# A two-layer decoder trunk on one core: compression input in two parts, MLP weights spread, first scores of layer 0 later, sparse-attention copies all on ScalarE

## The chip, the core and the metric

The kernel runs on one core of one Trainium2 chip. The metric is the device time of one execution in microseconds; the time before is the median of three runs. All detail comes from one further execution that was profiled.

## What is computed

x has 512 tokens of 1024 channels, in float32. Each of two layers normalises x, projects it to 5912 columns, runs two attentions side by side on the result, gates and merges them, and adds the output projection to x. Cut to what matters here:

```python
def hybrid_layer(x, pos, ...):
    h = rms_norm(x, norm_g)
    sb_q, sb_k, sb_v, sb_z, n_q, n_kc, n_vc, n_ks, n_vs, n_kw, n_vw, n_gate, n_z, gate_a, gate_b = split(h @ w_in)
    o_a = stick_breaking_attention(heads(sb_q), heads(sb_k), heads(sb_v))   # 8 heads
    y_a = merge_heads(o_a) * silu(sb_z)
    q = rope(rms_norm(heads(n_q)), pos)
    o_b = nsa_attention(q, ...)      # compressed, selected and window branches, 8 heads over 2 key groups
    y_b = o_b * silu(n_z)
    merged = sigmoid(gate_a) * (y_a @ w_up_a) + sigmoid(gate_b) * (y_b @ w_up_b)
    return x + merged @ w_out

def compress_blocks(x, idx, pe, w1, b1, w2):      # keys and values of the compressed branch
    blocks = x[:, :, idx] + pe                    # 31 blocks of 32 tokens, stride 16
    return silu(flat(blocks) @ w1 + b1) @ w2
```

Stick-breaking attention takes for each query the scores of earlier keys, a reversed cumulative sum of their log-sigmoids, and weights w from both. The sequence of 512 tokens is worked in blocks of 128 queries.

## The kernel before

A float32 product is split: a weight raw becomes whi (a rounded copy, from a cast on ScalarE or GpSimd) and wlo = raw - whi (on VectorE, line 408), the activations h become hh and hl, and TensorE adds three products, hh with whi, hl with whi and hh with wlo. So each projection is a row of matmuls of 512 columns, 24 for a block of 128 output columns, with raw loaded by SP's queue through a few rotating buffers (`w_load`, `w_split`, `w_get`). The matmuls of the value projections (`proj_tok`) go the other way round, with 256 columns.

The order of the work is written by a small planner while the program is built, in `Pacer`. It keeps a clock of its own in assumed microseconds; `pc.later(us, fn)` emits fn once that clock has advanced so far, and `pc.pump(us)` takes matmuls from a queue of fill work, `pc.fill`, until the clock has advanced by so much. The assumed delays are in `LAT`, `X_GAP`, `Y_GAP` and `Y_LAT`. On VectorE, ScalarE and GpSimd priorities (`tc.high_priority`) decide which of the instructions at hand goes first.

A layer has these stages.

- Start. In layer 0 x is loaded and transposed by TensorE into banks S; ScalarE copies them out (line 592), GpSimd and VectorE make hh and hl (lines 593, 594), and the first projections for stick-breaking (one pair of heads) run at once. r, the norm's factor, comes from a Ln and an Exp on ScalarE (lines 604, 605) and is broadcast into r_bc (line 621); a second Ln and Exp make an epsilon term (270, 271). sX and sK are the stacked operands of the scores; half of sK is moved to other partitions by a DMA that ScalarE issues (825, 826).
- X, the stick-breaking part. For t = 0 to 15, four heads' pairs times four query blocks, `sb_qk` makes the scores S, `sb_cs` the cumulative sums, and two steps later `sb_pv` makes the output o from w and the values gv. In each step ScalarE makes e = exp(S), its log, and w. Between these, fill work runs in the order of `X_FILL`: q, sq and sk are projections, cmp the two compressed projections, vs and vn the values, mlp 0 to 3 the four quarters of the compression MLP's hidden layer, k the keys of the sparse part. `LAT["sb0"]` is how long after the first projections the first scores are called for.
- `prep_cmp` (the cmp fill) evicts each projection into ct (line 687) and adds the position term pe to overlapping blocks, which gives f_t, the input of the compression MLP: per projection eight adds of 64 x 248 on VectorE (line 694), two key groups by two token parities by two halves of the block. `prep_mlp` multiplies f_t with the MLP weights (two loads per quarter). `prep_vs` evicts the values with VectorE into gv (line 663).
- Y, the sparse part. For u = 0 to 15 (four pairs of heads, j, times four query blocks, i), `nsa_qk` makes the scores of selected and window keys, VectorE their maxima mx (1047), ScalarE pr = exp (1052), VectorE scales pr (1060). `nsa_t` transposes pr on TensorE into tp and copies each block to SBUF as pT, blocks 0 and 2 on ScalarE (line 1074), 1 and 3 on VectorE (1076). `nsa_pv` multiplies pT with the values. Once per j, `cmp_qk` makes the compressed scores sc (to line 997), `cmp_t` transposes them and copies them to pcT on ScalarE (1006), and `cmp_pv` uses pcT. Gates and z projections are the fill here (`Y_FILL`).
- Merge and output projection, not touched.

The sine and cosine tables for the rotary embedding are made once, in layer 0, on ScalarE (`angles_sin`, lines 243 to 248). They need another table set of ScalarE than Exp and Ln do, so each Sin is ordered behind the last Ln instructions that the program has recorded so far in `lns`, and after them the Exp and Ln set is loaded by hand (line 141):

```python
sins = [A.activation(cos_t, cos_t, AF.Sin, bias=halfpi, scale=-1.0), ...]
for i in sins:
    for j in lns:
        order(i, j)
sin_tab.load, sin_tab.n = load_exp_ln(sins), 8
```

Where an instruction needs a set that is not active and nothing was loaded by hand, the compiler puts a load in (ACT_TABLE_LOAD with that instruction's line).

Of the kernel before, what the change touches and what calls it, by code (L numbers as in the profile page):

```python
# [17 lines left out]
AF = mybir.ActivationFunctionType  # L18
# [19 lines left out]
PRIO = 300  # L38
FIRST_R = 6
N_WARM = (3, 2, 2, 3)  # L40
LAT = {'norm': 5.0, 'mlp_t': 9.0, 'mlp_w2': 3.5, 'mlp_k': 16.0, 'sb0': 3.0, 'sb': 4.5, 'ang': 1.5, 'sin': 0.5}
PRIO_SB = 600
PRIO_EV = 900
X_GAP = (3.5, 3.4)
Y_GAP = 1.5
Y_LAT = (7.3, 6.9, 6.9, 8.8)
N_GATE = 13

# [2 lines left out]
def kernel(  # L51
# [20 lines left out]
    V, A, T, G = nc.vector, nc.scalar, nc.tensor, nc.gpsimd  # L72
# [54 lines left out]
    with tc.high_priority(offset=3000):  # L127
        pt = t_bank()
# [96 lines left out]
    def angles_load():  # L225
        pos_i = wk.tile([P, S], I32, tag="wk", name="pos_i")
        nc.sync.dma_start(pos_i, positions[0:1, :].to_broadcast([P, S]))
        pc.later(LAT["ang"], lambda: angles_reduce(pos_i))

# [116 lines left out]
    pc = Pacer()  # L346
# [170 lines left out]
    def tok_plan(l, p):  # L517
        return [("tok", l, p, 0), ("tok", l, p, 1)]

    X_FILL = [('q', 0), ('sq', 1), ('sk', 1), ('sq', 2), ('sk', 2), ('cmp', 0), ('vs', 1), ('mlp', 0), ('mlp', 1), ('sq', 3),  # L520
              ('sk', 3), ('k', 0), ('mlp', 2), ('k', 1), ('mlp', 3), ('vn', 0), ('q', 1), ('q', 2), ('q', 3)]
    Y_FILL = [("z", 0), ("g", 0), ("g", 1), ("g", 2), ("g", 3), ("z", 1), ("g", 4), ("g", 5), ("z", 2),
              ("g", 6), ("g", 7), ("z", 3)] + [("g", a) for a in range(8, N_GATE)]
# [118 lines left out]
    for l in range(depth):  # L642
# [3 lines left out]
        with ExitStack() as lc:  # L646
# [3 lines left out]
            done = set()  # L650
# [29 lines left out]
            def prep_cmp():  # L680
                for f in f_v:
                    V.memset(f[:, :, :, :, NCMP:], 0.0)
                for a, c in ((0, C_KC), (1, C_VC)):
                    po = yield from proj(l, "col", c)
                    ct = wkt("ct")
                    with tc.high_priority(offset=PRIO_EV):
                        V.tensor_mul(ct, po, r_bc)
                    for g in range(2):
                        gs = slice(g * HD, (g + 1) * HD)
                        pe_v = pe_t[gs, l, a].rearrange("p (k t) -> p k t", t=2)  # L690
                        for t in range(2):
                            src = ct[gs].rearrange("p (c k t) -> p k t c", k=8, t=2)
                            for hf in range(2):
                                V.tensor_tensor(  # L694
                                    f_v[hf][t * HD:(t + 1) * HD, :, a, g, 0:NCMP],
                                    src[:, :, t, hf:hf + NCMP],
                                    pe_v[:, hf * 8:(hf + 1) * 8, t:t + 1].to_broadcast([HD, 8, NCMP]),
                                    op=ALU.add)

            def prep_k(b):  # L700
                po = yield from proj(l, "col", (C_KS, C_KW)[b])
# [12 lines left out]
            mlp = H()  # L714
# [348 lines left out]
            def nsa_t(pr, i, gap):  # L1063
                pTs = []
                for kb in range(i + 1):
                    pt = t_bank()
                    ptv = pt.rearrange("p (g t q) -> p g t q", g=2, t=2)
                    for g in range(2):
                        for t in range(2):
                            tr(ptv[:, g, t], pr[g][:, kb, t], identf)  # L1070
                    pT = py.tile([P, 2, 2, P], F32, tag="pT", name="pT", bufs=NT)
                    with tc.high_priority(offset=PRIO_SB):
                        if kb % 2 == 0:
                            A.activation(pT.rearrange("p g t q -> p (g t q)"), pt, AF.Copy)  # L1074
                        else:
                            V.tensor_copy(pT.rearrange("p g t q -> p (g t q)"), pt)  # L1076
                    pTs.append(pT)
                    pc.pump(gap)
                return pTs
# [19 lines left out]
            with ExitStack() as lx:  # L1099
# [59 lines left out]
                eng.copy = copy_pool  # L1159
                sb_evac_q(R, po[0])  # L1160
                sb_evac_k(R, po[1])
                pc.later(LAT["sb0"], lambda: done.add(("sb", 0)))
                pc.fill.append(prep_vs(0))
                pc.fill.extend([fills[kind](a) for kind, a in X_FILL])
                NS = 4 * NT
# [18 lines left out]
            with ExitStack() as ly:  # L1184
                py = ly.enter_context(tc.tile_pool(name=f"py{l}", bufs=1, reuse_waits="tile"))
                pc.fill.extend([fills[kind](a) for kind, a in Y_FILL])
                sc = cmp_qk(0)
# [3 lines left out]
                for u in range(17):  # L1191
                    j, i = u // NT, u % NT
                    pc.pump(ready - pc.now)
                    if u > 0:
                        nsa_pv(o, pTs, (u - 1) % NT)
                        if i == 0:
                            nsa_o(j - 1, o)
                    if u == 16:
                        break
                    if u < 15:  # L1200
                        j2 = (u + 1) // NT
                        pc.until(lambda: j2 in n_in)
                        pr[u + 1] = nsa_qk(j2, (u + 1) % NT)
                        ready = pc.now + Y_LAT[(u + 1) % NT]
                        if i == 2 and j < 2:
                            pc.until(lambda: ("q", j + 2) in done)
                            set_nX(j + 2, n_q[j + 2])
                    if i == 0:
                        pcT = cmp_t(sc)
                    pTs = nsa_t(pr.pop(u), i, Y_GAP)  # L1210
                    if i == 0:
                        o = cmp_pv(pcT)
                    if i == 2 and j < 3:
                        pc.until(lambda: j + 1 in n_in)
                        sc = cmp_qk(j + 1)
# [110 lines left out]
```

## Time and profile before

| | |
|---|---|
| median of 3 runs | 1015.94 us (1014.74 to 1016.39) |
| the profiled execution | 1017.15 us, span 1015.4 us |
| TensorE busy | 980.1 us, 97%, 5379 matmuls |
| VectorE busy | 698.3 us, 69% |
| ScalarE busy | 444.9 us, 44% |
| GpSimd busy | 208.2 us, 21% |
| the chain that ended last | TensorE 75%, VectorE 16%, ScalarE 4%, DMA 2% |

The span is what the profile covers, from the first to the last instruction; the run's own time is 1.75 us longer. TensorE is PE in the profile, VectorE DVE, ScalarE ACT, GpSimd POOL. "Busy" counts a matmul to its modelled end, so neighbouring matmuls overlap; how fast TensorE works is better read from the distance of two starts.

### The profile page before, as it was taken

How to read it: one execution, taken by the hardware profiler on the slowest of the kernel's cores; microseconds unless marked ns; L12 is line 12 of the kernel's file. 1: busy time of each engine (PE TensorE's matmuls, PEld its weight loads, DVE VectorE, ACT ScalarE, POOL GpSimd, SP SyncE). 2: the span in 40 equal slices, each digit the busy share in tenths (PEclk: the TensorE clock that was granted, in tenths of full speed). 3: DMA queues.
4: the chain of work that ended last, by engine and by line, in shares of the span. 5: the costliest groups of instructions: out<-in, count | busy, mean ns of one | idle time of the engine just before them, and what ended most of it. 6: DMA issues, size and time to landing. Idle time of an engine off the chain costs nothing.

```text
span 1015.4 us, 14862 instructions
## 1 busy us (share of the span) xinstructions
PE 980.1 (97%) x5379; PEld 770.7 (76%) x5379; DVE 698.3 (69%) x1369; ACT 444.9 (44%) x1102; POOL 208.2 (21%) x256
## 2 busy tenths in 40 slices
PE   6999899999999999999999989999999999999997
PEld 5877767767777778888888776687777777788886
DVE  7778557889696876465565965687977776755631
ACT  4554446655243333623344533666534332345321
POOL 4152243621101101000014424352210110100000
PEclk9999899999999999999999989999999999999999
DMA  9333066432221212344643315463222121224341
GB/s 289 101 95 102 5 173 139 115 84 53 63 64 42 63 50 72 88 128 121 177 115 85 93 41 146 107 146 84 62 63 63 42 63 43 62 83 136 93 115 52
DMA packets 167530, 94.36 MB, mean 93 GB/s; under 512 B 39568, under 2 KB 160672, under 8 KB 167456
## 3 DMA queue, kind: packets, MB, share of 16 engines
q1 hardware_dynamic: 163120, 88.14, 32.3%
q10 hardware_dynamic: 3632, 3.17, 1.3%
q0 software_dynamic: 704, 2.11, 0.5%
q8 instruction: 42, 0.69, 0.3%
q14 instruction: 32, 0.26, 0.1%
HBM read 80.81 MB, written 6.29 MB: 86 GB/s over the span
## 4 chain that ended last, share of the span: by engine, by line
PE 75%; DVE 16%; ACT 4%; DMA 2%; issue 1%; POOL 1%; SPq 0%; DVEq 0%; POOLq 0%; ACTq 0%
PE acc L349 48%; PE S L349 16%; PE o L349 5%; PE tp L353 3%; DVE mx L1047 2%; DVE wlo L408 2%; DVE pr L1060 2%; ACT pr L1052 2%; PE tp L349 1%; DVE f_t L694 1%; DVE nX L509 1%; DMA raw<-in_w_in_dram 1%; DMA sK<-sK 1%; DMA mpos_i<-in_positions_dram 1%; DVE mx L1049 0%
## 5 line engine op out<-in xcount | busy, mean ns | idle before, releaser
L349 PE MATMUL acc<-hh,whi 128*128 128x512 f32 x640 | 256.9, 401 | 2.9 <-POOL whi L162 1.9
L349 PE MATMUL acc<-hl,whi 128*128 128x512 f32 x640 | 256.3, 401 | 1.7 <-DVE hl L594 1.4
L349 PE MATMUL acc<-hh,wlo 128*128 128x512 f32 x640 | 178.7, 402 | 0.0
L408 DVE TENSOR_TENSOR wlo<-raw,whi 128x1024 fp32r<-128x1024 f32 (+1 forms) x124 | 158.2, 1277 | 26.1 <-POOL whi L162 15.9
L162 POOL TENSOR_SCALAR whi<-raw 128x1024 fp32r<-128x1024 f32 (+1 forms) x84 | 98.5, 1174 | 374.3 <-PE acc L349 259.1
L349 PEld LDWEIGHTS acc<-hh,whi 128*128 128x128 f32 x640 | 121.2, 189 | 28.8 <-POOL whi L162 2.9
L349 PEld LDWEIGHTS acc<-hl,whi 128*128 128x128 f32 x640 | 120.9, 189 | 28.1 <-DVE hl L594 3.4
L349 PEld LDWEIGHTS acc<-hh,wlo 128*128 128x128 f32 x640 | 118.1, 189 | 26.5 <-issue 3.1
L408 ACT CAST whi<-raw 128x1024 fp32r<-128x1024 f32 x40 | 42.0, 1050 | 122.9 <-PE S L349 45.9
L1052 ACT ACTIVATE pr<-S,mx 128x256 f32<-128x256 f32 (+1 forms) x192 | 81.8, 446 | 32.0 <-DVE mx L1049 24.3
L1074 ACT ACTIVATE pT<-tp 128x512 f32<-128x512 f32 x48 | 28.7, 599 | 96.1 <-PE tp L353 95.8
L1047 DVE TENSOR_REDUCE mx<-S 128x2 f32<-128x512 f32 (+1 forms) x96 | 53.5, 594 | 20.6 <-PE S L349 20.4
L349 PE MATMUL acc<-whi,hh 128*128 128x256 f32 (+1 forms) x192 | 58.7, 306 | 6.0 <-DVE gv L663 6.0
L219 ACT ACTIVATE e<-S 128x128 f32<-128x128 f32 (+3 forms) x64 | 25.4, 435 | 86.6 <-DVE S L903 82.9
L353 PE MATMUL tp<-identf,pr 128*128 128x128 f32 x320 | 50.4, 278 | 9.4 <-DVE pT L1076 3.1
L349 PE MATMUL acc<-wlo,hh 128*128 128x256 f32 (+1 forms) x192 | 56.8, 296 | 0.0
L349 PE MATMUL acc<-whi,hl 128*128 128x256 f32 (+1 forms) x192 | 56.6, 295 | 0.0
L353 PEld LDWEIGHTS tp<-identf,pr 128*128 128x128 f32 x320 | 38.0, 141 | 21.8 <-ACT pcT L1006 6.5
L349 PE MATMUL S<-yh,wlo 128*128 128x512 f32 x128 | 50.8, 396 | 0.0
L349 PE MATMUL S<-yh,whi 128*128 128x512 f32 x128 | 50.7, 396 | 0.0
L1060 DVE TENSOR_SCALAR pr<-pr,rc 128x128 f32<-128x128 f32 (+3 forms) x128 | 49.3, 429 | 1.6
L349 PE MATMUL S<-yl,whi 128*128 128x512 f32 x128 | 50.1, 392 | 0.0
(315 smaller groups left out, 1784.3 us busy)
## 6 DMA issues: line engine op xcount, KB each, us to landing
raw<-in_w_in_dram SPq DMA_DIRECT2D x72, 512.0 KB, 3.8
raw<-in_w_in_dram SPq DMA_DIRECT2D x36, 256.0 KB, 3.8
raw<-in_cmp_w_dram SPq DMA_DIRECT2D x16, 512.0 KB, 4.4
raw<-in_w_out_dram SPq DMA_DIRECT2D x16, 512.0 KB, 4.0
raw<-in_w_up_a_dram SPq DMA_DIRECT2D x16, 256.0 KB, 3.1
raw<-in_w_up_b_dram SPq DMA_DIRECT2D x32, 128.0 KB, 3.3
gv<-xs SPq DMA_DIRECT2D x16, 256.0 KB, 2.7
sq<-xq SPq DMA_DIRECT2D x48, 64.0 KB, 2.0
```

The lines of the kernel that those rows point to most:

```text
L162: G.tensor_scalar(dst, src, 1.0, 0.0, op0=ALU.mult, op1=ALU.add)
L219: ins = A.activation(dst, src, func, **kw)
L349: T.matmul(out, lhsT, rhs, start=start, stop=stop, **kw)
L353: T.transpose(out, in_, ident)
L408: for ins in (eng.copy(hi, rv), V.tensor_sub(lo, rv, hi.bitcast(F32))):
L509: V.tensor_sub(X[b, g], q[a], X[a, g].bitcast(F32))
L694: V.tensor_tensor(f_v[hf][t * HD:(t + 1) * HD, :, a, g, 0:NCMP], src[:, :, t, hf:hf + NCMP], pe_v[:, hf * 8:(hf + 1) * 8, t:t + 1].to_broa ...
L1047: V.tensor_reduce(mx[:, hf, g], sbk[-1], axis=AX.XY, op=ALU.max, negate=True)
L1052: exps.append(A.activation(pr[g][:, a:b, t], sbk[hf][:, t], AF.Exp, bias=mx[:, 0, g, t:t + 1], accum_out=dn[:, hf, g, t:t + 1]))
L1060: V.tensor_scalar(pr[g][:, :nk, t], pr[g][:, :nk, t], rc[:, g, t:t + 1], None, op0=ALU.mult)
L1074: A.activation(pT.rearrange("p g t q -> p (g t q)"), pt, AF.Copy)
```

## The change

- `prep_cmp` emits the four adds of one key group's first half (`block(0)`) at once and those of the second half (`block(1)`) later, by a delay `F_GAP` on the planner's clock.
- In `X_FILL` the second MLP quarter goes behind the projection ('sq', 3).
- The first scores are called for after 6.0 instead of 3.0 in layer 0 and after 3.8 in layer 1.
- `nsa_t` copies every pT on ScalarE.
- `cmp_t` is called ahead of `nsa_pv` and `nsa_qk` instead of behind them.

```diff
-LAT = {'norm': 5.0, 'mlp_t': 9.0, 'mlp_w2': 3.5, 'mlp_k': 16.0, 'sb0': 3.0, 'sb': 4.5, 'ang': 1.5, 'sin': 0.5}
+LAT = {'norm': 5.0, 'mlp_t': 9.0, 'mlp_w2': 3.5, 'mlp_k': 16.0, 'sb0': 3.8, 'sb': 4.5, 'ang': 1.5, 'sin': 0.5}
+F_GAP = ((6.0, 8.0), (5.0, 7.0))
...
-    X_FILL = [('q', 0), ('sq', 1), ('sk', 1), ('sq', 2), ('sk', 2), ('cmp', 0), ('vs', 1), ('mlp', 0), ('mlp', 1), ('sq', 3),
+    X_FILL = [('q', 0), ('sq', 1), ('sk', 1), ('sq', 2), ('sk', 2), ('cmp', 0), ('vs', 1), ('mlp', 0), ('sq', 3), ('mlp', 1),
...
-                        for t in range(2):
-                            src = ct[gs].rearrange("p (c k t) -> p k t c", k=8, t=2)
-                            for hf in range(2):
+                        src = ct[gs].rearrange("p (c k t) -> p k t c", k=8, t=2)
+
+                        def block(hf, a=a, g=g, src=src, pe_v=pe_v):
+                            for t in range(2):
                                 V.tensor_tensor(
                                     f_v[hf][t * HD:(t + 1) * HD, :, a, g, 0:NCMP],
                                     src[:, :, t, hf:hf + NCMP],
                                     pe_v[:, hf * 8:(hf + 1) * 8, t:t + 1].to_broadcast([HD, 8, NCMP]),
                                     op=ALU.add)
+
+                        block(0)
+                        pc.later(F_GAP[a][g], lambda block=block: block(1))
...
-                        if kb % 2 == 0:
-                            A.activation(pT.rearrange("p g t q -> p (g t q)"), pt, AF.Copy)
-                        else:
-                            V.tensor_copy(pT.rearrange("p g t q -> p (g t q)"), pt)
+                        A.activation(pT.rearrange("p g t q -> p (g t q)"), pt, AF.Copy)
...
-                pc.later(LAT["sb0"], lambda: done.add(("sb", 0)))
+                pc.later(LAT["sb0"] if l else 6.0, lambda: done.add(("sb", 0)))
...
                     pc.pump(ready - pc.now)
+                    if i == 0 and u < 16:
+                        pcT = cmp_t(sc)
                     if u > 0:
                         nsa_pv(o, pTs, (u - 1) % NT)
...
-                    if i == 0:
-                        pcT = cmp_t(sc)
                     pTs = nsa_t(pr.pop(u), i, Y_GAP)
```

The change also moves instructions that it does not name. Three places follow; the line numbers of the changed kernel are one higher from line 46 on and up to five higher further down.

VectorE in layer 0, from the second compressed projection to the first eviction of values; f_t is the MLP's input in two tiles, ct the evicted projection, e a part of the stick-breaking scores. Before (the two kinds of add alternate four times where the dots stand):

```order
L903 TENSOR_TENSOR S<-S,mk_sb 128x128 x2
L687 TENSOR_TENSOR ct<-acc,r_bc 128x512
L907 SCALAR_TENSOR_TENSOR e<-S,e 128x384 x2
L694 TENSOR_TENSOR f_t_187<-ct,pe_t 64x8x31
L694 TENSOR_TENSOR f_t_188<-ct,pe_t 64x8x31
...
L663 TENSOR_SCALAR gv<-acc,r_col 128x256
L923 TENSOR_TENSOR sp<-e,sp 128x384 x2
L663 TENSOR_SCALAR gv<-acc,r_col 128x256
```

Now:

```order
L688 TENSOR_TENSOR ct<-acc,r_bc 128x512
L409 TENSOR_TENSOR wlo<-raw,whi 128x1024
L696 TENSOR_TENSOR f_t_187<-ct,pe_t 64x8x31 x2
L908 TENSOR_TENSOR S<-S,mk_sb 128x128 x2
L696 TENSOR_TENSOR f_t_187<-ct,pe_t 64x8x31 x2
L696 TENSOR_TENSOR f_t_188<-ct,pe_t 64x8x31
L664 TENSOR_SCALAR gv<-acc,r_col 128x256
L696 TENSOR_TENSOR f_t_188<-ct,pe_t 64x8x31 x2
L912 SCALAR_TENSOR_TENSOR e<-S,e 128x384 x2
L696 TENSOR_TENSOR f_t_188<-ct,pe_t 64x8x31
L664 TENSOR_SCALAR gv<-acc,r_col 128x256
```

All eight adds stood between ct and the first gv; now five do, with a wlo and an S pair, and three adds and the e pair follow gv.

ScalarE in layer 0's start, from the last cast of weights (whi) to the two transfers of sK; ssc and y hold the norm's factor. Before:

```order
L408 CAST whi<-raw 128x1024 x2
L604 ACTIVATE ssc<-ssc 128x4
L605 ACTIVATE ssc<-ssc 128x4
L621 COPY r_bc<-tp 128x512
L270 ACTIVATE y<-r_bc 128x512
L271 ACTIVATE y<-y,lneps 128x512
L508 ACTIVATE sX<-q 64x512
L825 ACTIVATE sK_197<-kk 64x512
L508 ACTIVATE sX<-q 64x512
L826 DMA sK_197<-sK_197 64x512
L825 ACTIVATE sK_197<-kk 64x512
L826 DMA sK_197<-sK_197 64x512
```

Now:

```order
L409 CAST whi<-raw 128x1024 x2
L605 ACT_TABLE_LOAD
L605 ACTIVATE ssc<-ssc 128x4
L606 ACT_TABLE_LOAD
L606 ACTIVATE ssc<-ssc 128x4
L622 COPY r_bc<-tp 128x512
L271 ACT_TABLE_LOAD
L271 ACTIVATE y<-r_bc 128x512
L272 ACT_TABLE_LOAD
L272 ACTIVATE y<-y,lneps 128x512
L509 ACTIVATE sX<-q 64x512
L830 ACTIVATE sK_197<-kk 64x512
```

Four ACT_TABLE_LOAD stand where there were none. A fifth new one stands further ahead, with the two small sines, between the Abs of cos_m and the first copies of x:

```order
L571 ACTIVATE gx,ssc<-x_sb_167 128x512
L245 ACTIVATE cos_m<-sin_m 64x32
L248 ACT_TABLE_LOAD
L248 ACTIVATE cos_m<-cos_m,halfpi 64x32
L571 ACTIVATE gx,ssc<-x_sb_168 128x512
L249 ACTIVATE sin_m<-sin_m 64x32
L593 COPY e<-S 128x512
```

Before, the small sines came after the first scores.

ScalarE in the sparse part of layer 0, third block of the first heads; pr are the exponentials, pT the copies. Before:

```order
L508 ACTIVATE nX<-gx 64x512 x2
L1074 ACTIVATE pT<-tp 128x512
L1052 ACTIVATE pr,dn<-S,mx 128x2x128 x6
L1074 ACTIVATE pT<-tp 128x512
L1052 ACTIVATE pr,dn<-S,mx 128x2x128 x2
L991 ACTIVATE sc<-sc 128x256
L1052 ACTIVATE pr,dn<-S,mx 128x128
L1074 ACTIVATE pT<-tp 128x512
```

Now:

```order
L509 ACTIVATE nX<-gx 64x512 x2
L1078 ACTIVATE pT<-tp 128x512
L1057 ACTIVATE pr,dn<-S,mx 128x2x128 x2
L1078 ACTIVATE pT<-tp 128x512
L1057 ACTIVATE pr,dn<-S,mx 128x2x128 x3
L1078 ACTIVATE pT<-tp 128x512
L1057 ACTIVATE pr,dn<-S,mx 128x2x128 x3
L996 ACTIVATE sc<-sc 128x256
L1057 ACTIVATE pr,dn<-S,mx 128x128
L1078 ACTIVATE pT<-tp 128x512
```

Two of the copies that VectorE had now stand among the exponentials, the first one behind two of them.

## Rows read from the trace of the kernel before

**Rows 1.** The page: busy time of each engine, share of the span, instructions.

```profile
PE 980.1 (97%) x5379; PEld 770.7 (76%) x5379; DVE 698.3 (69%) x1369; ACT 444.9 (44%) x1102; POOL 208.2 (21%) x256
```

**Rows 2.** Waits of PE by releaser: us in total, times, longest us.

```profile
PE acc L349 <- DVE gv L663: 6.0, 2, 3.0
...
PE tp L353 <- DVE pT L1076: 3.1, 4, 0.9
PE tp L353 <- DVE pr L1060: 3.0, 4, 0.9
PE tp L353 <- ACT pcT L1006: 2.8, 6, 0.5
PE acc L349 <- POOL whi L162: 1.9, 2, 1.0
...
PE S L349 <- DVE sK L827: 1.3, 2, 1.1
PE tp L353 <- DVE sc L997: 1.2, 2, 0.6
PE S L349 <- ACT e L905: 1.1, 1, 1.1
```

**Rows 3.** Timeline of PE, layer 0: start us, us, engine, line, operation, [idle before].

```profile
104.80 0.28 PE L349 MATMUL acc<-whi,hl 128*128 128x256 f32 x1
...
106.92 0.28 PE L349 MATMUL acc<-whi,hl 128*128 128x256 f32 x1
110.22 0.58 PE L349 MATMUL acc<-whi,hh 128*128 128x256 f32 x1 [3.02 <-DVE gv L663]
...
113.95 0.41 PE L349 MATMUL acc<-whi,hh 128*128 128x256 f32 x1
...
116.30 0.40 PE L349 MATMUL acc<-whi,hl 128*128 128x256 f32 x1
```

**Rows 4.** Windows: us; PE, PEld, DVE, ACT, POOL busy (x); PEclk; DMA share; GB/s.

```profile
38.05:41.46 3.41, 3.41 (x16) 3.41 (x17) 2.72 (x8) 2.84 (x8) 0.70 (x2) 0.50 0.00 0
109.73:116.56 6.83, 6.34 (x24) 4.74 (x25) 2.36 (x6) 2.38 (x5) 0.00 (x0) 0.50 0.00 0
601.25:608.08 6.83, 6.80 (x26) 5.19 (x27) 1.90 (x5) 2.84 (x6) 0.00 (x0) 0.50 0.00 1
```

**Rows 5.** Timeline of DVE in layer 0, and the page's group of wlo (busy, mean ns).

```profile
101.59 0.69 DVE L687 TENSOR_TENSOR ct<-acc,r_bc 128x512 f32<-128x512 f32 x1
...
104.62 5.03 DVE L694 TENSOR_TENSOR f_t<-ct,pe_t 64x248 f32<-64x248 f32 x8
...
L408 DVE TENSOR_TENSOR wlo<-raw,whi 128x1024 fp32r<-128x1024 f32 (+1 forms) x124 | 158.2, 1277 | 26.1 <-POOL whi L162 15.9
```

**Rows 6.** Timeline of SP's queue and of POOL; the page's DMA issues (KB, us to landing).

```profile
125.10 1.00 SPq L366 DMA_DIRECT2D raw<-in_w_in_dram  x2
...
129.08 1.04 POOL L162 TENSOR_SCALAR whi<-raw 128x1024 fp32r<-128x1024 f32 x1 [1.99 <-DMA raw<-in_w_in_dram]
...
raw<-in_cmp_w_dram SPq DMA_DIRECT2D x16, 512.0 KB, 4.4
```

**Rows 7.** Groups by line and form: busy, mean ns of one, idle before.

```profile
L1074 ACT ACTIVATE pT<-tp 128x512 f32<-128x512 f32 x48 | 28.7, 599 | 96.1 <-PE tp L353 95.8
...
L1076 DVE COPY pT<-tp 128x512 f32<-128x512 f32 x32 | 22.0, 688 | 16.9 <-PE tp L353 16.7
...
L1052 ACT ACTIVATE pr<-S,mx 128x256 f32<-128x256 f32 (+1 forms) x192 | 81.8, 446 | 32.0 <-DVE mx L1049 24.3
```

**Rows 8.** Timeline of ACT and its queue; the page's issues of sK.

```profile
33.92 0.48 ACTq L826 DMA_DIRECT2D sK<-sK  x1
...
39.88 1.28 ACT L247 ACT_TABLE_LOAD   x1
41.17 0.32 ACT L247 ACTIVATE cos_m<-cos_m,halfpi 64x32 f32<-64x32 f32 x1
...
sK<-sK ACTq DMA_DIRECT2D x16, 128.0 KB, 2.3
```

## The prediction

> **What bounds the kernel now.** I read the page first. TensorE is busy 980.1 of 1015.4 us and its matmul count does not change, so there are two things to win or lose: the 35 us in which it has nothing to run, and the stretches in which its granted clock is not full [rows 1]. VectorE, at 69%, and ScalarE, at 44%, matter only where TensorE waits for them. So the second view was TensorE's waits by releaser. The reader is to see that a few names carry them: gv 6.0, pT 3.1, pr 3.0, pcT 2.8, whi 1.9, and the first scores' sK and e with 1.3 and 1.1 [rows 2]. The third was TensorE's own timeline at the largest of them: the matmul of 106.92 is followed by one at 110.22, and from there matmuls of the same shape start every 0.21 us instead of every 0.12 [rows 3]. The fourth was a table of stretches, which shows the clock at 0.50 for 6.83 us behind each of the two gv waits, and for 3.41 us at the first scores of layer 0 [rows 4]. Half is the lower of the two levels, 1.2 GHz. Each gv wait is therefore paid twice.
>
> **The change, term by term.** All terms are against the profiled execution, 1017.15 us, which is 1.2 above the median of the runs.
>
> *Compression input in two parts.* Before, ct ends at 102.28, VectorE then idles and runs one e pair, and all eight adds to f_t (5.03 us, 0.63 each) stand between them and gv; gv ends just before 110.22 [rows 3, 5]. In the new order of layer 0 one wlo (1.28 us [rows 5]), one S pair and five adds stand between ct and gv, and the e pair comes later. Counted from ct's end: 1.3 for wlo, 3.1 for five adds, about 0.5 each for the S pair and gv, together 5.4 us. Before, ct's end to gv's end took 7.9. TensorE's question came 107.2 - 102.3 = 4.9 us after ct's end. In the new order 12 + 36 short matmuls of the same 48 and one o and S group lie in between, where before it was a group of cumulative sums; by these lengths the question comes 5.5 to 6.5 us after ct's end, so gv is ready with up to 1 us to spare. In layer 1 only wlo, the e pair and one add stand ahead, and there is more room. Both waits go: 110.22 - 106.92, less the pitch of 0.12, is 3.18 each, **6.35**. With them goes what the clock took: TensorE was busy 6.34 and 6.80 us there at half clock [rows 4], and at a pitch of 0.118 (104.80 to 106.92, 18 steps) for 0.214 (113.95 to 116.30, 11 steps) [rows 3] that is 45% too long: 2.85 + 3.05 = **5.9**. What it costs if the cover fails is below, as a rival.
>
> *MLP weights spread.* The load of sq's weights left the queue only at 125.10, when the first MLP quarter had freed its buffer; the whi made from it, a step of 1.04, waited for it until 129.08 [rows 6], and TensorE for the whi, 1.9 us over the two layers [rows 2]; with the pipeline's refill of about 0.2 each, **2.3**. In the new fill order the sq projection comes ahead of the second MLP quarter, so its load has a buffer early. The load that is now late, the quarter's second half, is issued at the same moment and needed one whole projection later (24 matmuls of 512 columns, over 5 us, with scores and cumulative sums between them), where such a load takes 4.4 [rows 6]. Nothing takes the place of this wait.
>
> *pT copies all on ScalarE.* 32 copies leave VectorE, where one took 0.688 us, for ScalarE, where one takes 0.599 [rows 7]. The waits put down to VectorE's pT (3.1, plus refill, 4 waits and some short ones: 4.3) came from its queue. In the new order the copy stands behind two of ScalarE's exponentials, 0.45 each [rows 7], not behind all six, so I leave 0.4 of each of the four: gain **2.7**. The other side: 32 x 0.6 = 19 us more on ScalarE, ahead of exponentials that feed pr. The four pr waits [rows 2] are places with no slack, and one copy ahead of each makes it 0.6 longer: **-2.4**. Bounds 0 and -4.8 (two copies ahead).
>
> *Compressed scores' transposes earlier.* For three of four heads per layer the copy pcT now has the o matmuls to run under: of the six waits, 2.8 us in all [rows 2], each costs 0.29 when the step from start to start is set against an undisturbed one of its shape: **1.75**. At the first head of each layer sc is asked for earlier. There TensorE already waits, for sc 1.2 us over the two layers and behind it for pr [rows 2]; pr now stands behind more VectorE work, and walking that queue gives about 0.5 us more in layer 0 and nothing in layer 1: **-0.5**. Bounds 0 and -1.3, one wlo [rows 5].
>
> *First scores of layer 0 delayed, start-up.* This is the part that speaks against the change. While the first scores are waiting no Ln has been recorded, so the sines find nothing to be ordered behind, and ScalarE's order has them among the first copies of x. Every Ln and Exp until the next load by hand then brings a table load of its own: 13 loads in the program where there were 8. One takes 1.28 us, and the next instruction starts at 41.17 where the load ended at 41.16 [rows 8]. First, the load and the two sines ahead of the first e copy (1.28, then 0.32 for the one shown [rows 8] and less for the other) delay a chain without slack: -1.7. Of the two loads for r, one is behind the last cast, the other stands on the path to r_bc: -1.2. Two more stand between r_bc and sK. The second sK transfer, issued at 33.92 [rows 8], then goes out 5.5 us later, about 39.4, and lands 2.3 later or, by its slowest, 4: 41.7 to 43.4. TensorE, with 27 short matmuls (3.15 us) put ahead of these scores, asks at about 41.3. So 0.4 to 2.1 remain of the 2.8 us that the first scores now wait (sK, e and refill, [rows 2]): +1.6. The 3.41 us at half clock here [rows 4], worth 1.5, go or stay at even odds: +0.75. Together **-0.55**, between -2.5 and +2.6.
>
> On what a load costs the row speaks first: 1.28 us with no gap on either side [rows 8]. The Trainium skill, "ScalarE: Activation LUTs", section "What ACT_TABLE_LOAD costs", gives the same load about 1.28 us but adds a drain of about 1.38, some 2.66 in all for every switch; by that page the four exposed loads would cost 5.5 us more than I count. The trace agrees on the load and shows no drain, so the sum goes by the row.
>
> *End of X.* The delayed scores shift the schedule by 3.15 us, so the fill of layer 0 runs out ahead of the last weights w, and TensorE stands there for about one ScalarE step: **-0.6**, by the length of a pT copy [rows 7]; bounds 0 and -1.2.
>
> Sum: 6.35 + 5.9 + 2.3 + 2.7 - 2.4 + 1.75 - 0.5 - 0.55 - 0.6 = 14.95. 1017.15 - 14.95 = 1002.2, and at the median, 1.2 lower, **1001.0 us**.
>
> **The rivals.**
>
> A. *The costs are covered* (ScalarE has room, the delayed scores meet their sK). Then -2.4, -0.5 and -0.6 vanish and start-up gives +2: 21 us, about **995**. For it: ScalarE idles over half of the time. Against: the five loads stand in the order. Chance 0.10.
>
> B. *gv is still late in one layer.* The spare us in layer 0 hangs on one wlo, which itself needs its whi; if that comes 2 us late TensorE waits 1 to 2 us, and the half-clock stretch may return: 1.5 + 2.9 given back, about **1005.5**. Chance 0.12.
>
> C. *A table switch costs more than the load*: the pipe is empty before and after it, as no row here shows. Were each of the four exposed loads to cost twice its 1.28, the start would lose 5.1 more and the half-clock stretch stay: about **1007**. This is the rule of the Trainium skill's page named above. Chance 0.06.
>
> D. *Slower: ScalarE's queue as the server of all pT.* In VectorE's place a copy would wait for all six exponentials of the next scores, 6 x 0.45 = 2.7 us [rows 7], where it now waits for one or two VectorE steps of 0.7: each of the 32 moved copies could come over 1 us later than before. At 1.1 us each that is 35 us against 14.65 from the rest (the sum without both pT terms), some **1036**; it decides from 13 or 14 such copies on. Against: the order puts the copy after two, three or four exponentials, and there are 12 to 24 matmuls between a transpose and its use. Chance 0.04.
>
> E. *The change does not do what it says*: block 1 is queued by the planner's clock, and could fall ahead of gv again if the planner's delays were short. The order has at least three of the eight behind gv in both layers. The sum without its first two terms gives about **1013**. Chance 0.02.
>
> **How the numbers follow.** The forecast, within 3.5 us of 1001, has 0.66; A 0.10, B 0.12, C 0.06, D 0.04, E 0.02. The bounds of the unknown costs (pr -4.8 to 0, start-up -2.5 to +2.6, first head, end of X) reach about 5 us either way when they fall together; the range takes in those, A's near half, and B and C: 996 to 1007. A measurement here can tell about 0.2%, 2 us, from no change. Faster by more: the forecast, A, B and C, 0.94; within: E, 0.02; slower: D, 0.04.
>
> **What would show it.** In the changed profile: no wait of TensorE for gv over 0.5 us, and no half-clock stretch near 110 or 600; no wait for whi at the end of the first MLP quarter; pT only on ScalarE, with waits for pr at 3 to 6 us; pcT waits nearly gone; 13 table loads, the first extra one just after 11.5 us, and the first scores near 40 us instead of 35 with 0.4 to 2.1 us of waits. Wrong would be: a half-clock stretch anywhere that was full before, TensorE waiting for ScalarE's pT in many places, or first scores after 44 us.

## The result, and the profile after

The changed kernel takes 1006.92 us (median of 4 runs, 1005.86 to 1008.56) where the kernel before takes 1015.97: a ratio of 0.992, 95% interval 0.991 to 0.994, some 8 to 9 us. The forecast was 15, to 1001.0. The direction was right; the size was off by six to seven microseconds, and, as the experiments show, 12 of the 15 us were put down to a part of the change that brings nothing by itself.

The waits of TensorE in the changed kernel, in microseconds in total, times, longest:

```profile
...
PE acc L350 <- DVE gv L664: 3.4, 4, 1.2
PE tp L350 <- DVE kC L807: 2.7, 1, 2.7
PE tp L354 <- DVE mlp_u L749: 2.6, 1, 2.6
PE tp L354 <- DVE pr L1065: 2.3, 2, 2.1
PE S L354 <- ACT e L593: 2.0, 1, 2.0
PE o L350 <- ACT w L220: 1.5, 2, 1.2
PE tp L354 <- DVE sc L1002: 1.4, 1, 1.4
PE tp L350 <- DVE dg L614: 1.2, 1, 1.2
...
PE S L350 <- DMA sK<-sK: 0.9, 1, 0.9
```

Against [rows 2] the reader sees that pT, pcT and whi are gone altogether and gv has fallen from 6.0 to 3.4 with none longer than 1.2. In their place stand names that were not there: kC 2.7, mlp_u 2.6, a w of 1.5 for the outputs o, and dg at the start, where the wait for the first copies e grew from 0.7 to 2.0. The 0.9 for sK is in layer 1, at 570 us. The w waits stand early in layer 0, at 80.65 and 92.15 us, far ahead of mlp_u (177.94) and kC (210.98):

```profile
80.65 0.54 PE L350 MATMUL o<-w,gv 128*64 128x384 f32 x1 [1.18 <-ACT w L220]
```

The clock shows the same. The two stretches of 6.83 us at half clock and the one of 3.41 us at the first scores [rows 4] are gone. So is a fourth, which [rows 4] does not list; it stood behind a pr wait at the start of layer 1's sparse part:

```profile
717.30:720.72 3.42, 3.25 (x10) 2.77 (x11) 3.42 (x9) 2.10 (x3) 0.00 (x0) 0.50 0.30 60
```

Two new ones of 3.41 us came: one in the start, behind the wait of 2.0 us for e, and one in the window about the mlp_u wait:

```profile
14.71:18.12 3.41, 3.41 (x13) 2.44 (x12) 2.99 (x3) 2.37 (x6) 3.41 (x5) 0.50 1.22 303
100.00:125.00 25.00, 24.00 (x167) 19.22 (x167) 19.08 (x36) 9.23 (x20) 6.94 (x11) 1.00 0.21 60
175.00:182.00 7.00, 4.41 (x22) 4.21 (x23) 5.71 (x13) 3.78 (x10) 2.91 (x4) 0.76 0.48 107
600.00:625.00 25.00, 23.88 (x141) 17.45 (x141) 16.20 (x32) 12.38 (x29) 5.21 (x8) 1.00 0.33 88
```

To see where the time went, one can use that both kernels run the same 5379 matmuls. For each matmul I took the undisturbed step of its shape, the median distance from its start to the next, and added these up; so much "work" is done at any moment. Then the time at which the changed kernel has done a given amount is set against the kernel before. Worked out in this way from the starts of the matmuls:

| stage (until, in the kernel before) | forecast | changed - before | in this stage |
|---|---|---|---|
| start of layer 0 (46.5 us) | +0.55 | -0.8 | -0.8 |
| X of layer 0 (218.8) | -6.6 | +4.9 | **+5.7** |
| Y and the rest of layer 0 (434.3) | -0.5 | -0.45 | **-5.35** |
| X of layer 1 (712.2) | -7.4 | -4.0 | -3.6 |
| Y and the rest of layer 1 | -1.0 | -10.55 | **-6.5** |

The start came out near the forecast. X of layer 0 lost where it was to win: 2.6 us go up to 102 us, where the w waits stand, 4.4 are won from there to 160, where gv and whi had kept TensorE, and 7.5 are lost from 160 on. X of layer 1 won half, and Y, for which 1.5 had been counted, won 12, the stretch at 717.30 included.

### The profile page after: what moved, and what is told of

It is laid out like the page before. It is cut to its first block, busy times and chain, and to the rows that moved or that the text cites. A ratio compares the mean times of both kernels' runs of the same rounds, so it can differ in the third digit from the quotient of the medians.

```text
span 1004.1 us, 14937 instructions
## 1 busy us (share of the span) xinstructions
PE 974.6 (97%) x5379; PEld 768.9 (77%) x5379; DVE 682.9 (68%) x1337; ACT 467.4 (47%) x1139; POOL 210.1 (21%) x256
## 4 chain that ended last, share of the span: by engine, by line
PE 67%; DVE 6%; issue 2%; ACT 2%; POOL 0%; DMA 0%; SPq 0%; DVEq 0%; ACTq 0%; POOLq 0%
PE acc L350 42%; PE S L350 15%; PE o L350 5%; PE tp L354 4%; PE tp L350 1%; DVE f_t L696 1%; DVE wlo L409 1%; ACT e L220 1%; DVE sp L928 0%; POOL whi L163 0%; DVE sq L500 0%; ACT e L910 0%; DVE sX L510 0%; PE S L354 0%; DVE sK L832 0%
## 5 line engine op out<-in xcount | busy, mean ns | idle before, releaser
L163 POOL TENSOR_SCALAR whi<-raw 128x1024 fp32r<-128x1024 f32 (+1 forms) x84 | 95.5, 1136 | 395.1 <-PE acc L350 323.7
L409 DVE TENSOR_TENSOR wlo<-raw,whi 128x1024 fp32r<-128x1024 f32 (+1 forms) x124 | 154.9, 1249 | 31.6 <-POOL whi L163 21.6
L1078 ACT ACTIVATE pT<-tp 128x512 f32<-128x512 f32 x80 | 48.0, 600 | 132.5 <-PE tp L354 132.0
L1065 DVE TENSOR_SCALAR pr<-pr,rc 128x128 f32<-128x128 f32 (+3 forms) x128 | 51.4, 444 | 1.4
```

Of the source, the lines that this page charges most:

```text
L163: G.tensor_scalar(dst, src, 1.0, 0.0, op0=ALU.mult, op1=ALU.add)
L409: for ins in (eng.copy(hi, rv), V.tensor_sub(lo, rv, hi.bitcast(F32))):
L1065: V.tensor_scalar(pr[g][:, :nk, t], pr[g][:, :nk, t], rc[:, g, t:t + 1], None, op0=ALU.mult)
```

## Experiments

All are compared with the kernel before on the same chip. Where an experiment says "8 table loads", the sines are emitted once an Ln has been recorded:

```diff
     def angles_sin():
+        if not lns:
+            pc.later(1.0, angles_sin)
+            return
```

**1. The delay in layer 0 undone.** The changed kernel with

```diff
-                pc.later(LAT["sb0"] if l else 6.0, lambda: done.add(("sb", 0)))
+                pc.later(LAT["sb0"] if l else 3.0, lambda: done.add(("sb", 0)))
```

> The changed kernel with one part undone: the first scores of layer 0 are called for after 3.0 again (layer 1 keeps 3.8). Theory P (the later scores of layer 0 put the chains of the stick-breaking part against the fill work in a bad place): the new waits of TensorE in layer 0 for mlp_u (2.6 us, with a half-clock stretch of 1.5 behind it), kC (2.7), w (1.5) and pr (2.1) go, about 9 us; the sines come after the first scores again with 8 table loads, and the start is back to before's, about 1 us slower than the changed kernel there. 997 to 1000 us. Rival R (the two-part input, the spread MLP weights or the copies on ScalarE make those waits): they stay, 1005 to 1008 us.

Measured: 999.17 us, ratio 0.985 (0.983 to 0.987). The waits for mlp_u and kC are gone and pr is down to 0.2, as theory P says; one gv wait of 2.4 us with its half-clock stretch is back in layer 0. So one of the five parts of the change, with the table loads that come with it, costs over 7 us.

**2. The table loads undone, the delay kept.** The edit above on the changed kernel.

> The changed kernel with the sines emitted only once an Ln has been recorded (the delay of 6.0 stays): 8 table loads instead of 13. Rival Q (the five loads at the start set everything in layer 0 late against the DMAs and the fill): start faster by 2 to 4 us and part of the mlp_u, kC and w waits gone, 998 to 1003 us. Theory P: the start is faster by 2 to 3 us, the waits for mlp_u, kC and pr stay, 1003 to 1005 us.

Measured: 1003.75 us, ratio 0.989 (0.987 to 0.991). The start gains 3.6 us by the comparison of work, and its half-clock stretch at 14.71 is gone; the waits for kC (2.7), mlp_u (2.6), pr (2.4) and w (1.5) stay as they are. Theory P: the five loads cost some 3 us by themselves and have no part in the later waits.

**3. The delay alone.** The kernel before with 6.0 in layer 0.

> The kernel before with one part of the change alone: the first scores of layer 0 after 6.0. 13 table loads. Theory P: waits for mlp_u, kC or w of several us appear in layer 0 here too, and the sum is 1018 to 1026 us. Rival R: only the start differs, by under 1 us in either direction, 1014 to 1017 us.

Measured: 1019.91 us, ratio 1.0055 (1.0033 to 1.0077). The page of waits shows what the kernel before did not have:

```profile
PE acc L349 <- DVE gv L663: 4.5, 3, 3.0
...
PE tp L349 <- DVE kC L802: 2.7, 1, 2.7
PE tp L353 <- DVE mlp_u L744: 2.6, 1, 2.6
...
PE o L349 <- ACT w L219: 1.5, 2, 1.2
```

kC, mlp_u and w are the waits of the changed kernel, to the tenth. But the long gv wait (3.0) is in layer 1 only. Where layer 0 had the other, 0.3 us is left: the delay has freed it, without the two-part input.

**4. The two-part input alone**, on the kernel before (the `block` lines of the diff and `F_GAP`).

> The kernel before with the compression input in two parts and nothing else. The prediction's first two terms: both gv waits (6.35 us) and both half-clock stretches (5.9 us) go, 1003 to 1006 us. Rival R (this part makes the mlp_u wait by putting the second halves in VectorE's way later): new waits of 3 to 6 us in layer 0, 1008 to 1011 us.

Measured: 1017.12 us, ratio 1.0016 (1.0002 to 1.0029). Both theories are wrong: there are no new waits of that kind, and no gain either, rather a loss of 0.2%. VectorE's timeline in layer 0:

```profile
103.87 0.69 DVE L688 TENSOR_TENSOR ct<-acc,r_bc 128x512 f32<-128x512 f32 x1
105.95 1.02 DVE L912 SCALAR_TENSOR_TENSOR e<-S,e 128x384 f32<-128x384 f32 x2 [1.39 <-POOL sp L963]
106.89 5.33 DVE L696 TENSOR_TENSOR f_t<-ct,pe_t 64x248 f32<-64x248 f32 x8
112.25 0.48 DVE L664 TENSOR_SCALAR gv<-acc,r_col 128x256 f32<-128x256 f32 x1
```

ct, 1.39 us of idle time, the e pair, eight adds without a break, gv: the order of the kernel before. The planner calls for the second halves later, but with 3.0 before the first scores nothing else comes forward that would go between, and e still stands ahead of all adds. The gv waits are 7.4 us in total, where they were 6.0; the profiled execution, at 1019.69 us, is the slowest of ten.

**5. The change without the two-part input.** All eight adds are emitted at once; the rest as changed.

> The changed kernel without the two-part input: the eight adds of a projection are emitted at once, as before; everything else changed. Theory S (the moment of the first scores against the fill, and with it what stands between ct and gv, frees gv; the split does little): gv waits as in the changed kernel (3.4 us in all, none over 1.5), 1005 to 1009 us. Theory F (the split frees gv, as the prediction has it): a gv wait of 3 us with its half-clock stretch comes back in at least one layer, 1011 to 1019 us.

Measured: 1007.33 us, ratio 0.991 (0.990 to 0.993), against 0.992 for the whole change: no difference that can be told, with gv waits of 2.8 us in total and none over 1.2. Theory S. The prediction's first two terms, 12.25 us, do not belong to the part that they were put down to.

**6. The MLP weights alone.**

> The kernel before with the MLP weights spread (the second quarter behind the projection sq 3) and nothing else. The prediction's term: the whi waits go, 2.3 us, and gv is still late with its half-clock stretches: 1012.5 to 1014 us. Theory M (in the new fill order a wlo and five adds, not eight, stand ahead of gv, so this part also shortens the gv waits, from 3.0 to about 2.3 each): 1010 to 1012 us. If it alone frees gv: 1001 to 1004 us.

Measured: 1010.61 us, ratio 0.995 (0.994 to 0.997). whi is gone from the waits and gv falls to 4.1 (2.1 the longest): theory M. The new fill order puts a wlo between ct and gv and takes three adds from there, which is what the two-part input was thought to do: in layer 0 ct ends at 103.77, a wlo, the e pair and five adds follow, and gv starts at 109.60.

**7. The moment of the first scores alone**: 3.8 in both layers, 8 table loads, on the kernel before.

> The kernel before with the first scores of both layers after 3.8 instead of 3.0, the sines emitted once an Ln has been recorded (8 table loads), and nothing else. Theory S (the moment of the first scores frees gv: four adds and the e pair stand ahead of it, and adds fill VectorE's idle 1.4 us before e): gv waits under 0.5 us, no half-clock stretch behind them, whi waits as before: 1003 to 1006 us. Rival (it takes the fill order as well): gv waits of 1 to 3 us with stretches, 1009 to 1015 us.

Measured: 1007.36 us, ratio 0.993 (0.991 to 0.996). gv is not among TensorE's waits any more, in neither layer, and the windows 100 to 125 and 600 to 625 us have the full clock:

```profile
100.00:125.00 25.00, 23.63 (x171) 19.20 (x170) 19.10 (x37) 12.62 (x30) 7.61 (x13) 1.00 0.27 76
600.00:625.00 25.00, 25.00 (x141) 18.11 (x141) 16.36 (x26) 11.61 (x30) 10.65 (x14) 1.00 0.58 169
```

```profile
103.30 0.69 DVE L690 TENSOR_TENSOR ct<-acc,r_bc 128x512 f32<-128x512 f32 x1
104.03 1.69 DVE L697 TENSOR_TENSOR f_t<-ct,pe_t 64x248 f32<-64x248 f32 x3
105.75 1.02 DVE L910 SCALAR_TENSOR_TENSOR e<-S,e 128x384 f32<-128x384 f32 x2
106.80 0.76 DVE L697 TENSOR_TENSOR f_t<-ct,pe_t 64x248 f32<-64x248 f32 x1
107.59 0.48 DVE L666 TENSOR_SCALAR gv<-acc,r_col 128x256 f32<-128x256 f32 x1
```

Three adds now run where VectorE idled, and e follows without a wait. Of the forecast's 12.25 us for freeing gv, 0.8 us of delay in the call for the first scores brings most, by itself: by the comparison of work 4.1 us are won between 100 and 125 and 7.5 between 590 and 625, a whi wait of 1 us included. It also removes the whi waits, which the expectation had kept. Other waits take a part back: ct 1.3, sq from 0.3 to 1.9, pcT from 2.8 to 3.8.

**8. The copies alone.**

> The kernel before with all pT copies on ScalarE and nothing else. The prediction's term: pT waits 4.3 us gone but for 1.6, pr waits 2.4 us longer, so about 1015.5 us, no change. Rival (the copies on VectorE also held up the scaling of pr, so both kinds of wait go): 6 to 8 us less, 1008 to 1010 us.

Measured: 1010.85 us, ratio 0.995 (0.993 to 0.997). pT is gone from the waits and pr stands at 3.1 in four waits, where [rows 2] has 3.0. So the gain, 5.0 us, is near the 4.3 us of the waits removed, and neither the -2.4 that I subtracted nor the 1.6 that I left is there.

**9. The transposes of the compressed scores alone.**

> The kernel before with the transposes of the compressed scores ahead of the o and S matmuls, and nothing else. The prediction's term: 1.75 us gained at three heads per layer, 0.5 lost at the first, 1014.5 us. Rival (the six waits cost their full 2.8 us, and the pr waits behind them go too): 1011 to 1013 us. Rival the other way (TensorE waits longer for sc at the first head of each layer than it saves): 1016 to 1019 us.

Measured: 1007.92 us, ratio 0.993 (0.991 to 0.994). More than any of the theories gave:

```profile
PE tp L353 <- DVE sc L997: 3.8, 2, 1.9
...
PE tp L353 <- DVE pT L1076: 1.1, 2, 0.6
```

pcT (2.8) and pr (3.0) are gone, pT has fallen from 3.1 to 1.1, and sc has risen from 1.2 to 3.8. TensorE's order in this part is different over a whole head, so copies and scalings have more matmuls to run under than those of the pcT copy; the comparison of work gives 2.0 us for layer 0's Y and 3.1 for layer 1's. An estimate from the waits: they are 4.8 us less in total and eleven fewer, which at the refill of some 0.2 us each is 7 us. Why exactly pr no longer waits was not traced.

**10. How much delay, and how long for the MLP.** Four kernels, all the changed kernel with 8 table loads: 3.8 in layer 0; 4.6; 4.6 in both layers; 4.6 with 11 us for the MLP's transposes (`mlp_t`, 9 before).

> The changed kernel with 3.8 in layer 0 too, and the sines emitted once an Ln has been recorded (8 table loads). Theory P with S: layer 0 then runs like layer 1 of the changed kernel: no waits for mlp_u, kC or w of over 1.5 us, and a gv wait of about 1.2 us without a half-clock stretch, where 3.0 left 2.4 us and a stretch of 2.7: 993 to 997 us. Against it: 3.8 delays the first scores in a layer whose start has other loads in flight, and waits as with 6.0 appear: 1000 to 1004 us.

> The changed kernel with 4.6 in layer 0 (not 6.0) and 8 table loads. If the loss in layer 0 grows with the delay: 999 to 1002 us, with some of the mlp_u, kC and w waits. If it sets in only near 6.0: 994 to 997 us.

> The changed kernel with 4.6 in both layers and 8 table loads. If the moment of the first scores acts in layer 1 as in layer 0 (ct wait of 2.2 and gv wait of 1.1 us in layer 1 fall to 0.7): 993 to 996 us. If layer 1 has other transfers and fill against it: 996 to 999 us.

> The changed kernel with 4.6 in layer 0, 8 table loads, and 11 us for the MLP's transposes. Theory K: its mlp_u wait of 1.3 us goes, 994.5 to 996 us. If the chain behind it (kC, cmp) then comes late for the sparse part: 996 to 998 us.

Measured: 998.26 us (ratio 0.983, 0.981 to 0.984), 996.13 (0.982, 0.980 to 0.984), **994.78** (0.981, 0.979 to 0.983) and 994.93 (0.982, 0.979 to 0.984). In the first, layer 0 has no wait for mlp_u or kC, but a ct wait of 2.2 us with a half-clock stretch behind it came, which had not been expected. Most of the loss of 6.0 sets in between 4.6 and 6.0; at 4.6 an mlp_u wait of 1.3 us is there already. In the fourth mlp_u's wait is gone, but a w of 1.4 in layer 0 and a kC of 1.3 in layer 1 have come. The last three can't be told apart from these runs; all three are faster than both kernels. What is left in the third:

```profile
PE tp L357 <- DVE sc L1005: 2.7, 2, 1.4
PE tp L357 <- DVE mlp_u L752: 2.6, 2, 1.3
PE tp L357 <- DVE sq L488: 2.3, 2, 1.2
PE acc L353 <- DVE gv L667: 1.4, 2, 0.8
```

No stretch of it runs at half clock.

**11. The first head as before** (`cmp_t` at u = 0 behind `nsa_qk`; 3.8 in both layers, 8 table loads).

> The changed kernel with 3.8 in both layers, 8 table loads, and at the first head of each layer (u = 0) the compressed scores' transposes where they were before. The prediction's step that the first heads lose 0.5 by the move: sc waits fall from 2.7 to about 1.2 us, pr or pcT waits behind them come back with about 1.5 us: 997 to 999 us, no difference from 998.3 that can be told. If the move costs its 1.5 us more there: 996 to 997 us.

Measured: 999.92 us, ratio 0.986 (0.984 to 0.988), where 998.26 stood without this; it lies above both forecasts. sc is gone, pr (1.7 in six waits) and pcT (0.9) are back. The move costs nothing at the first heads; what sc waits for longer is given back behind it.

**12. Why mlp_u is late at 6.0.** The changed kernel with 8 table loads, 6.0, and

```diff
-LAT = {... 'mlp_t': 9.0, ...}
+LAT = {... 'mlp_t': 12.0, ...}
```

> The changed kernel with 8 table loads, the delay of 6.0 kept, and the MLP's transposes called for 12 us instead of 9 after the last quarter's sum. Theory K (with 6.0 the sum meets ScalarE and VectorE while they work through the k projection's norm and the next scores, so its chain takes over 10 us where the planner allows 9): the mlp_u wait of 2.6 us and the half-clock stretch of 1.4 behind it go: 999 to 1001 us, with the kC wait moved or kept. Rival (the chain is late because TensorE's own order holds it up): the wait moves along with the transposes, 1003 to 1005 us.

Measured: 1005.57 us, ratio 0.992 (0.989 to 0.994), no better than the 1003.75 of experiment 2. The wait for mlp_u is gone, as theory K says, but the time is not won:

```profile
PE o L353 <- ACT w L220: 3.7, 3, 2.1
...
PE tp L353 <- DVE kC L810: 2.7, 1, 2.7
```

w has taken its place, with 3.7 instead of 1.5: a new wait of 2.1 us at 182.40. It is not TensorE's own order, since the wait did not move with the transposes, and not the planner's 9 alone. Nor is ScalarE too busy for this w; it had stood idle:

```profile
180.10 1.28 ACT L715 ACTIVATE kN<-sq 64x512 fp32r<-64x512 f32 x2 [3.33 <-DVE sq L504]
```

In ScalarE's order this kN step of the k projection stands ahead of w, and it waits for sq, which VectorE comes to at 178.51, behind the copies of the MLP's transposes. So, as far as this trace shows, TensorE waits for the order in which the two streams share both queues, at whichever name it asks for first. Theory K is right about the late chain and wrong about what its planned delay is worth. The timelines of the kernel before and of the changed kernel show the chain. In the kernel before, VectorE starts on the last quarter's sum at 171.47 and on the finished mlp_u at 174.46:

```profile
171.47 0.41 DVE L734 TENSOR_TENSOR mlp_u<-acc,mlp_u 128x256 f32<-128x256 f32 x1
...
173.52 0.42 DVE L158 SCALAR_TENSOR_TENSOR e<-mlp_u,e 128x256 f32<-128x256 f32 x1 [0.64 <-ACT e L219]
...
174.46 0.42 DVE L744 TENSOR_TENSOR mlp_u<-mlp_u,e 128x256 f32<-128x256 f32 x1
```

and in the changed kernel at 167.30 and 177.46. VectorE, then ScalarE:

```profile
167.30 0.41 DVE L739 TENSOR_TENSOR mlp_u<-acc,mlp_u 128x256 f32<-128x256 f32 x1
...
175.37 1.34 DVE L159 SCALAR_TENSOR_TENSOR e<-mlp_u,e 128x256 f32<-128x256 f32 x1 [0.34 <-ACT e L220]
...
177.46 0.42 DVE L749 TENSOR_TENSOR mlp_u<-mlp_u,e 128x256 f32<-128x256 f32 x1
```

```profile
170.34 0.58 ACT L220 ACTIVATE w<-S 128x512 f32<-128x512 f32 x1
...
171.33 0.59 ACT L220 ACTIVATE w<-S 128x512 f32<-128x512 f32 x1
...
172.79 0.63 ACT L712 ACTIVATE kN<-sq 64x512 fp32r<-64x512 f32 x1
173.33 0.40 ACT L156 ACTIVATE e<-mlp_u 128x256 f32<-128x256 f32 x1
...
174.16 0.42 ACT L157 ACTIVATE e<-e 128x256 f32<-128x256 f32 x1 [0.43 <-ACT e L156]
...
176.74 0.42 ACT L160 ACTIVATE e<-e 128x256 f32<-128x256 f32 x1 [0.82 <-DVE e L159]
```

From the first start to the last end, 3.4 us have become 10.6, over the planner's 9. ScalarE's fixed order has two weights w and the kN step of the k projection ahead of the first step on mlp_u, and other steps of k, of the values and of the scores between its own.

The kC wait meets other work. VectorE's two short kC steps empty the bank that TensorE asks for, and each stands behind a long step for the cumulative sums, the first also behind the norm of the next projection:

```profile
208.88 0.17 DVE L807 TENSOR_TENSOR kC<-tp,kC 64x32 fp32r<-64x32 f32 x1
208.98 1.64 DVE L928 TENSOR_TENSOR spl<-e,sph 128x512 fp32r<-128x512 f32 x1
210.64 0.19 DVE L807 TENSOR_TENSOR kC<-tp,kC 64x32 fp32r<-64x32 f32 x1
```

## Why the prediction was wrong, step by step

*The sum.* That the total came within seven microseconds is in part luck. By the table the two X stages came out 16 us worse than forecast and the start and Y 12 us better.

*Bounds.* Right: what the kernel could win were TensorE's waits and the half-clock stretches. The version with 4.6 in both layers has none of the latter, and is 20 us faster than the kernel before.

*Compression input in two parts: 6.35 + 5.9.* The step failed in its cause. "All eight adds ahead of gv, now five" was read from the order of the whole change, and the change in the order was put down to the edit that names f_t. By experiments 4 and 5 that edit brings nothing, by 6 and 7 the fill order and the moment of the first scores do. Its size failed too. In layer 0 both half-clock stretch and wait went, but TensorE asked for gv 4.4 us after ct's end and not 5.5 to 6.5, and gv was done after 4.8 (5.4 said); so gv still kept TensorE 0.5 us twice and 1.2 us at the first values, up to 40.30 us, and in layer 1 a wait of 1.1 stayed, which I had given "more room".

*MLP weights: 2.3.* Right for the waits, and 5.2 us as a part by itself, as it also shortens the gv waits.

*pT on ScalarE: 2.7 - 2.4.* Wrong in both halves: 5.0 was won by the part alone and nothing paid. The 0.6 per pr wait assumed that a copy stands ahead of each late pr on a ScalarE without slack; no pr wait grew.

*Compressed transposes: 1.75 - 0.5.* Undersized. I counted only the step from sc to pr, 0.29 each, and not the waits for pr and pT around it; the part by itself brings 7.9 us between medians. The loss at the first heads is not one (experiment 11).

*Start-up: -0.55.* Right within 1.4 us in the sum: 13 table loads, the second sK transfer at 38.66 (39.4 said), the first scores at 41.57. In its parts it was not. Of the 0.4 to 2.1 us that these scores were to wait, nothing is left, and the half-clock stretch behind them is gone; against that stand the gv wait of 1.2 at 40.30 and the new stretch at 14.71, which had not been counted. The loads cost about 3 us (experiment 2), which the delay's gain covered. Rival C, that a switch costs more than the load, is refuted here:

```profile
32.37 1.28 ACT L271 ACT_TABLE_LOAD   x1
33.66 0.64 ACT L271 ACTIVATE y<-r_bc 128x512 f32<-128x512 f32 x1
34.32 1.28 ACT L272 ACT_TABLE_LOAD   x1
35.62 0.72 ACT L272 ACTIVATE y<-y,lneps 128x512 f32<-128x512 f32 x1
```

Each load takes 1.28 us, the next step follows 0.01 to 0.02 us later and the second load starts 0.02 after the step before. "ScalarE: Activation LUTs" of the Trainium skill, section "What ACT_TABLE_LOAD costs", adds a drain of 1.38; no row shows it.

*End of X: -0.6.* This is the step that cost the forecast. I moved the scores of layer 0 by 3.15 us against the fill and asked only where the fill runs out. The chains that hang on both now meet other work: the MLP's activation the k projection's norm on ScalarE and VectorE, kC the cumulative sums and the next norm on VectorE. In the changed kernel that is 2.6 + 2.7 us of waits and 1.5 us of half clock (by the comparison of work 7.5 us from 160 us on), with an allowance of 0.6 against it. Its upper bound of 1.2 was the length of two steps, while what was to be bounded was a chain of seven steps on two engines. The last weights w, for which the 0.6 stood, are not among the waits there. The delay's other loss has no term at all: the two w waits at 80.65 and 92.15, 2.6 us by the comparison of work. They come with 6.0 (experiments 2 and 3 have them) and not with 4.6; what makes them late was not traced.

*The rivals.* None was it. Of A both conditions came true, no pr wait was added by the copies and the delayed scores met their sK, but the gain did not. C's number, 1007, is the measured time by luck: its mechanism is refuted above. B's 1005.5 is near by luck as well: it is about a late chain in layer 0, but about gv, whose half-clock stretch did not return. Of E half is true: the later call for block 1 decides nothing (experiment 5), yet the waits that it was to free went all the same. Two of the signs of being wrong appeared, half-clock stretches at 14.71 and 178.55, where the clock had been full.

## What to carry to other kernels

A new order belongs to the whole change; before a gain is put down to one edit, print the order with that edit alone. Here the edit that names the bottleneck did nothing, and one number that shifts two streams of work against each other by 0.8 us did what it was meant to do, while 3 us in layer 0 lost more than it won. When such a shift is made, walk every chain that joins the two streams with the queues of all engines on it, not only the place where the streams end.

## What the runs showed of the hardware

A VectorE step took three times its time while GpSimd worked. The step e of the mlp_u chain took 0.42 us in the kernel before, with GpSimd idle. In the changed kernel it started at 175.37 and took 1.34, and GpSimd's step ran from 175.16 to 176.43:

```profile
175.16 1.27 POOL L499 TENSOR_TENSOR yy<-xq,cos_t 128x512 f32<-128x512 f32 x1 [4.17 <-DVE xq L492]
```

VectorE's step ended 0.28 us after GpSimd's did. The Trainium skill, "SBUF — State Buffer", section "SBUF: two separate sides", says that a VectorE step with two SBUF inputs and a GpSimd step that reads SBUF hold a shared port pair in turn, each for its whole length; the numbers agree with that, though no run took the GpSimd step away.

How long TensorE runs at half clock differs between runs of one kernel, and with it the time. The forty runs of the kernel before that stand beside the experiments reach from 1011.7 us, at a granted clock of 0.996 over the run, to 1017.6 us, at 0.989. The version of experiment 10 that has no half-clock stretch stayed within 994.69 to 994.93 us in its four runs, at 0.999 to 1.000. The term of 5.9 us was read from one execution, at 0.989, near the low end of the clock.
